# A hybrid layer whose engine queues are ordered by the scheduler's finer timeline model

## The chip, the cores and the metric

The kernel runs on one core of one Trainium2 chip. A core has engines that each work through a queue of their own, in order, and meet at semaphores: PE (TensorE, the matmuls), DVE (VectorE), ACT (ScalarE), POOL (GpSimd) and SP (SyncE, which here only issues DMA transfers). The metric is the device time of one launch in microseconds (us), the median over runs.

## The reference

One decoder layer, batch 1, 1024 tokens, width 1024, all float32. A cut of it:

```
def _hybrid_layer(x, ...):
    xn = _rmsnorm(x, norm1_g)
    proj = xn @ w_in                          # q, k, v (8 heads of 64) and u (512)
    q, k = _rmsnorm(q, q_norm_g), _rmsnorm(k, k_norm_g)
    attn = _dilated_attention(q, k, v)        # windows 128/512/2048, dilations 1/4/16
    ssm = _s5_mixer(u, ...)                   # 32 groups, 64 complex states each, then GELU and a gate
    mix = jnp.concatenate([_rmsnorm(attn, attn_out_norm_g), _rmsnorm(ssm, ssm_out_norm_g)], axis=-1)
    x = x + mix @ w_out
    hdn = jnp.square(jax.nn.relu(_rmsnorm(x, norm2_g) @ w_mlp_up))   # 1024 x 4096
    return x + hdn @ w_mlp_down                                      # 4096 x 1024
```

## The kernel before

Every large matrix product is made of three matmuls, because a float32 operand is split in a high and a low part: `split` (L76 to L78) writes the high part on ACT and then the low part on DVE, and `mm3` (L103 to L107) issues high by high (L105), high by low (L106) and low by high (L107), where "low" of the third is that of the operand which PE holds as weights. The first two matmuls of a product can therefore start when ACT has written the high part of the weights; the third needs DVE's low part.

The stages, in the order in which PE comes to them in the profile (times from the start of the span):

- 0 to about 73 us: the projection of u for 8 tiles of 128 tokens, beside the S5 parameters on DVE.
- to 222 us: the S5 mixer, in four quarters q. `ssm_main` loads a table D from d_kz (L393, on SP), makes psb on PE (L399), scans on DVE (L417), forms X (L425, L429; two of its products on POOL, L424 and L428), and sums psy on PE from D by U (L435) and X by ec (L438). GELU follows (L445 to L451, ending in z2), then a transpose (pszt, L461), a copy hz (L462) and a write to d_hz (L463, on SP). Woven into it is the projection of the first pair of heads: psq, 24 matmuls for each token tile and group of columns.
- 222 to 433 us: attention of pair p-1 beside the projection psq of pair p, for p from 1 to 3. In attention, pss are scores (L541), psp their transposes (L564), pt the split of these (L77 on ACT, L78 on DVE) and pso the product with V (L575).
- to 594 us: attention of the last pair, the gate, the output projection and the operands X0 to X6 of the MLP (t1 to t4 on L815 are sums that these are made of).
- 594 to about 892 us: the up projection in 16 blocks (`up_proj`, L853 to L920). A block loads its weights as two raw buffers of 512 KB (wm of the block, parts 0 and 1, L853 on SP), of which there are only two in all: part 0 of a block goes where part 0 of the block before was, as soon as that has been read for the last time. A block has seven products of 12 matmuls, in the order z, x, first y, T2 (into x's bank), B22 (into y's), T3 and T4 (into x's). Each takes one half of a tile wu for its split weights; five such tiles go round. L897, L902, L906 and L911 form the sums of weights on DVE, in place; T3's weights are the last that are read from part 0. After x, first y and T2 ACT copies the bank (L871, st from psx or psy), since later products add onto it.
- 892 to 1219 us: the down projection, on the same engines (`down_proj`; raw, ud, L969 to L980).

The order in the program text is not the order in the queues. The tile framework takes the instructions of the whole kernel, with their dependencies, and a scheduler in it lists them for each engine in the order in which its model of the engines says that they become ready. So the cost model of that scheduler is what sets the queues. Nothing changes at run time: an engine takes its list in order, and waits where the next instruction isn't ready.

## Time and profile before

| | us |
|---|---|
| median of 3 runs | 1217.33 (1213.23 to 1218.86) |
| the profiled execution | 1220.95 |
| its span (first to last instruction) | 1219.2 |

The profiled execution is 3.6 us above the median; 1.75 us of it lie outside its span. PE is the busiest engine, with 1139.4 us of the span. The rows further down come from this execution, and times in them count from the start of its span. "Busy" of PE is modelled, so a PE that is busy throughout may still run at half its clock: the granted clock stands in its own row or column (1.00 is 2.4 GHz, 0.50 is 1.2 GHz).

### The profile page before, as it was taken

How to read it: one execution, taken by the hardware profiler on the slowest of the kernel's cores; microseconds unless marked ns; L12 is line 12 of the kernel's file. 1: busy time of each engine (PE TensorE's matmuls, PEld its weight loads, DVE VectorE, ACT ScalarE, POOL GpSimd, SP SyncE). 2: the span in 40 equal slices, each digit the busy share in tenths (PEclk: the TensorE clock that was granted, in tenths of full speed). 3: DMA queues.
4: the chain of work that ended last, by engine and by line, in shares of the span. 5: the costliest groups of instructions: out<-in, count | busy, mean ns of one | idle time of the engine just before them, and what ended most of it. 6: DMA issues, size and time to landing. Idle time of an engine off the chain costs nothing.

```text
span 1219.2 us, 16630 instructions
## 1 busy us (share of the span) xinstructions
PE 1139.4 (93%) x5734; PEld 956.7 (78%) x5734; DVE 841.0 (69%) x1557; ACT 598.6 (49%) x1276; POOL 354.8 (29%) x528
## 2 busy tenths in 40 slices
PE   6766989999999999999999999999999999999998
PEld 4554777888898877787777888888878888888887
DVE  7999785567676777666876566665656775576763
ACT  5222233677776786533555555555544333333332
POOL 6685642354545445313312111122110000000000
PEclk9886887899999999999999999999999999999999
DMA  7734432635355425753244434434379999575930
GB/s 288 272 115 106 151 112 70 211 114 178 129 155 170 143 96 166 243 191 121 75 159 173 167 145 165 145 140 167 144 294 398 387 387 352 193 240 183 333 140 35
DMA packets 101093, 227.15 MB, mean 186 GB/s; under 512 B 8848, under 2 KB 27792, under 8 KB 96144
## 3 DMA queue, kind: packets, MB, share of 16 engines
q1 hardware_dynamic: 85136, 154.13, 37.2%
q0 software_dynamic: 14432, 69.22, 15.7%
q10 hardware_dynamic: 1440, 2.73, 0.6%
q8 instruction: 45, 0.74, 0.3%
q14 instruction: 40, 0.33, 0.1%
HBM read 168.93 MB, written 57.11 MB: 185 GB/s over the span
## 4 chain that ended last, share of the span: by engine, by line
PE 70%; DVE 11%; DMA 6%; issue 5%; POOL 4%; ACT 4%; SPq 0%; ACTq 0%; DVEq 0%; POOLq 0%
PE psx L105 7%; PE psx L106 7%; PE psx L107 7%; PE psy L105 7%; PE psy L106 7%; PE psy L107 7%; PE pso L575 3%; PE psq L107 2%; PE psq L105 2%; PE psq L106 2%; PE pss L541 2%; PE psp L564 2%; PE psy L438 1%; PE pso L107 1%; PE pso L105 1%
## 5 line engine op out<-in xcount | busy, mean ns | idle before, releaser
L77 ACT ACTIVATE ud<-raw 128x1024 fp32r<-128x1024 f32 x112 | 112.9, 1053 | 184.8 <-PE psy L107 81.0
L78 DVE TENSOR_TENSOR ud<-raw,ud 128x1024 fp32r<-128x1024 f32 x112 | 132.6, 1221 | 83.6 <-ACT ud L77 83.6
L105 PE MATMUL psx<-X,wu 128*128 128x512 f32 (+1 forms) x260 | 101.1, 389 | 4.5 <-ACT st L871 3.2
L106 PE MATMUL psx<-X,wu 128*128 128x512 f32 (+1 forms) x260 | 100.4, 386 | 0.7 <-DVE X L78 0.7
L107 PE MATMUL psx<-X,wu 128*128 128x512 f32 (+1 forms) x260 | 100.5, 386 | 0.5 <-DVE wu L78 0.5
L105 PE MATMUL psy<-ud 128*128 128x512 f32 x256 | 99.6, 389 | 0.0
L106 PE MATMUL psy<-ud 128*128 128x512 f32 x256 | 99.6, 389 | 0.0
L107 PE MATMUL psy<-ud 128*128 128x512 f32 x256 | 99.6, 389 | 0.0
L78 DVE TENSOR_TENSOR wu<-wm,wu 128x512 fp32r<-128x512 f32 x112 | 75.5, 701 | 30.8 <-ACT wu L77 30.6
L105 PE MATMUL psq<-wq,xt 128*128 128x384 f32 x256 | 93.7, 366 | 0.9 <-DMA xt<-d_x 0.8
L77 ACT ACTIVATE wu<-wm 128x512 fp32r<-128x512 f32 x112 | 66.7, 625 | 53.1 <-DMA wm<-in_w_up_dram 27.0
L106 PE MATMUL psq<-wq,xt 128*128 128x384 f32 x256 | 90.6, 354 | 0.5 <-DVE wq L82 0.5
L107 PE MATMUL psq<-wq,xt 128*128 128x384 f32 x256 | 90.8, 355 | 0.0
L875 POOL DMA_DIRECT2D d_a<-st x80 | 43.5, 544 | 130.1 <-DVE st L884 65.9
L106 PE MATMUL psx<-ud 128*128 128x512 f32 x192 | 74.8, 390 | 0.0
L105 PE MATMUL psx<-ud 128*128 128x512 f32 x192 | 74.7, 389 | 0.0
L107 PE MATMUL psx<-ud 128*128 128x512 f32 x192 | 74.7, 389 | 0.0
L980 DVE TENSOR_TENSOR raw<-raw 128x1024 f32<-128x1024 f32 x40 | 49.7, 1249 | 28.7 <-DMA raw<-in_w_down_dram 28.7
L549 POOL TENSOR_SCALAR s<-s,dn 128x128 f32<-128x128 f32 (+3 forms) x64 | 50.2, 787 | 47.9 <-DVE dn L548 45.9
L78 DVE TENSOR_TENSOR pt<-psp,pt 128x128 fp32r<-128x128 f32 (+2 forms) x96 | 51.1, 552 | 15.9 <-ACT pt L77 15.2
L105 PEld LDWEIGHTS psx<-X,wu 128*128 128x128 f32 x260 | 48.8, 188 | 16.5 <-ACT st L871 4.6
L575 PE MATMUL pso<-pt,V 128*128 128x256 f32 x320 | 54.6, 294 | 3.5 <-ACT pt L77 1.9
(294 smaller groups left out, 3012.5 us busy)
## 6 DMA issues: line engine op xcount, KB each, us to landing
raw<-in_w_down_dram SPq DMA_DIRECT2D x96, 512.0 KB, 9.0
xt<-d_x POOLq DMA_DIRECT2D x30, 1024.0 KB, 5.2
raw<-d_a SPq DMA_DIRECT2D x56, 512.0 KB, 8.1
d_a<-st POOLq DMA_DIRECT2D x80, 256.0 KB, 2.6
wm<-in_w_up_dram SPq DMA_DIRECT2D x32, 512.0 KB, 3.7
d_x<-xt POOLq DMA_DIRECT2D x8, 1024.0 KB, 5.1
d_a<-o POOLq DMA_DIRECT2D x32, 256.0 KB, 2.8
wq_r<-in_w_qkv_dram SPq DMA_DIRECT2D x16, 384.0 KB, 3.9
```

What stands on the lines that cost most here:

```text
L77: ACT.activation(h, src, AF.Copy)
L78: eng.tensor_tensor(l, src, h.bitcast(F32), op=OP.subtract)
L105: PE.matmul(ps, lhsT=ah, rhs=bh, start=start, stop=False, skip_group_check=more)
L106: PE.matmul(ps, lhsT=ah, rhs=bl, start=False, stop=False, skip_group_check=more)
L107: PE.matmul(ps, lhsT=al, rhs=bh, start=False, stop=stop, skip_group_check=more)
L438: PE.matmul(psy[s][:, a], lhsT=X[s * 64:s * 64 + 64, ri, a, :], rhs=ca[s * 64:s * 64 + 64, ri, a].rearrange("p d c -> p (d c)"), start=Fal ...
L541: PE.matmul(ps[:, :cw], lhsT=Qd[a][:, h, b * 128:(b + 1) * 128], rhs=K2[:, h, c0:c0 + cw], start=a == 0, stop=a == 1)
L549: POOL.tensor_scalar(s[:, :n], s[:, :n], dn, 1.0, op0=OP.mult, op1=OP.mult)
L564: PE.transpose(ps[:, kb * 128:(kb + 1) * 128], P[j][:, (k0 + kb) * 128:(k0 + kb + 1) * 128], ident)
L575: PE.matmul(po[:, :256], lhsT=V2[:, k0 + kb, h, :], rhs=pt[:, a, kb, :], start=k0 + kb == 0 and a == 0, stop=k0 + kb == nb - 1 and a == 1)
L875: POOL.dma_start(out=d_a[blk // 2][i][blk % 2], in_=st)
L980: DVE.tensor_tensor(rb, rb, raw_unit(wd(n, *b1)), op=op)
```

## The change

```
-    with tile.TileContext(nc) as tc:
+    with tile.TileContext(nc, schedule_with_timeline_sim=True) as tc:
         hybrid_layer_kernel(tc, io, out)
```

The scheduler uses another, finer model of the engines. The instructions are the same ones (5487 matmul rows on PE, 1557 on DVE, 1076 on ACT, 528 on POOL, 385 on SP, before and now), with the same shapes and dependencies; 4825 of PE's stand at another place in its queue (by up to 158 places), 1265 of DVE's, 735 of ACT's, 341 of POOL's and 143 of SP's. Buffer addresses can differ too. Three places follow.

PE in the up projection, block 4 (psx_7085 is its x, psx_6796 the x bank of block 2, psx_6940 that of block 3). Before, x of block 4 begins behind the last product (T4) of block 3:

```order
L105 MATMUL psx_6940<-X5_6001,wu_7063 128x512
L106 MATMUL psx_6940<-X5_6002,wu_7063 128x512
L107 MATMUL psx_6940<-X5_6001,wu_7063 128x512
L105 MATMUL psx_7085<-X0_5284,wu_7063 128x512
L106 MATMUL psx_7085<-X0_5285,wu_7063 128x512
L107 MATMUL psx_7085<-X0_5284,wu_7063 128x512
L105 MATMUL psx_7085<-X0_5284,wu_7063 128x512
```

Now it begins between T3 (weights wu_6854) and T4 (weights wu_6904) of block 2:

```order
L105 MATMUL psx_6796<-X6_5993,wu_6854 128x512
L106 MATMUL psx_6796<-X6_5994,wu_6854 128x512
L107 MATMUL psx_6796<-X6_5993,wu_6854 128x512
L105 MATMUL psx_7085<-X0_5284,wu_7063 128x512
L106 MATMUL psx_7085<-X0_5285,wu_7063 128x512
L105 MATMUL psx_6796<-X5_6001,wu_6904 128x512
L106 MATMUL psx_6796<-X5_6002,wu_6904 128x512
```

So the first product of block 4 moved from the end of block 3 to before the last product of block 2, and everything of block 3 that stood between now comes later.

ACT at the same place, where the rows read the same before and now (st_6851 is the copy of T2 of block 2, wm3_0 and wm3_1 the weights of block 3, wm4_0 those of block 4):

```order
L871 ACTIVATE st_6851<-psx_6796 128x512
L77 ACTIVATE wu_7020<-wm3_0_6899 128x512
L880 ACTIVATE st_6851<-st_6851 128x512
L881 ACTIVATE st_6851<-st_6851 128x512
L77 ACTIVATE wu_7063<-wm3_1_6901 128x512
L77 ACTIVATE wu_7063<-wm4_0_7044 128x512
```

That is the copy, the last read of wm3_0 on ACT, and, once wm4_0 has landed in its place, the split for x of block 4. These did not move among themselves; only PE's use of wu_7063 moved against them.

PE at the end of the S5 mixer (psq_1938 is a projection of the first pair of heads, psy0_1841 the last quarter's sum, X_1769 its X). Before, the projection is dealt out among the sums:

```order
L105 MATMUL psq_1938<-wq0_0_916,xt_1936 128x384
L106 MATMUL psq_1938<-wq0_0_916,xt_1936 128x384
L107 MATMUL psq_1938<-wq0_0_916,xt_1936 128x384
L438 MATMUL psy0_1841<-ec_1344,X_1769 128x128
L105 MATMUL psq_1938<-wq0_0_916,xt_1936 128x384
L106 MATMUL psq_1938<-wq0_0_916,xt_1936 128x384
L107 MATMUL psq_1938<-wq0_0_916,xt_1936 128x384
L438 MATMUL psy0_1841<-ec_1344,X_1769 128x128
```

Now all 24 of its matmuls stand ahead of the first sum with X_1769:

```order
L105 MATMUL psq_1938<-wq0_3_937,xt_1936 128x384
L106 MATMUL psq_1938<-wq0_3_937,xt_1936 128x384
L107 MATMUL psq_1938<-wq0_3_937,xt_1936 128x384
L438 MATMUL psy0_1841<-ec_1344,X_1769 128x128 x2
L435 MATMUL psy0_1841<-D_1723,U3_1643 128x128
L438 MATMUL psy0_1841<-ec_1344,X_1769 128x128 x2
```

Of psq_1938, 21 matmuls moved from behind that sum's start to before it.

DVE at the start of the up projection (t1, t2, t4, X1, X2 and X5 are operands of the last token tiles, raw_8782 a tile of the down projection, wm0 and wm1 the weights of blocks 0 and 1). Before:

```order
L815 TENSOR_TENSOR t1_6443<-psx_6428,b11s_6439 128x512
L906 TENSOR_TENSOR wm0_1_6465<-wm0_1_6465,wm0_0_6463 128x512
L815 TENSOR_TENSOR t2_6445<-psx_6434,t1_6443 128x512
L78 TENSOR_TENSOR wu_6530<-wm0_0_6463,wu_6530 128x512
L815 TENSOR_TENSOR t4_6447<-psx_6422,t2_6445 128x512
L78 TENSOR_TENSOR X2_5770<-psx_6434,X2_5769 128x512
L78 TENSOR_TENSOR wu_6565<-wm0_1_6465,wu_6565 128x512
L78 TENSOR_TENSOR X1_5380<-psx_6422,X1_5379 128x512
```

Now:

```order
L911 TENSOR_TENSOR wm0_0_6463<-wm0_1_6465,wm0_0_6463 128x512
L78 TENSOR_TENSOR wu_6530<-wm0_0_6463,wu_6530 128x512
L980 TENSOR_TENSOR raw_8782<-raw_8782,raw_8785 128x1024
L800 SCALAR_TENSOR_TENSOR xsn_6405<-x2_6359,rs2_6412,g2b_5723 128x512
L800 SCALAR_TENSOR_TENSOR xsn_6406<-x2_6360,rs2_6412,g2b_5723 128x512
L78 TENSOR_TENSOR wu_6565<-wm0_1_6465,wu_6565 128x512
L78 TENSOR_TENSOR wu_6615<-wm0_1_6465,wu_6615 128x512
L78 TENSOR_TENSOR wu_6565<-wm0_0_6463,wu_6565 128x512
L815 TENSOR_TENSOR t1_6443<-psx_6428,b11s_6439 128x512
L815 TENSOR_TENSOR t2_6445<-psx_6434,t1_6443 128x512
L78 TENSOR_TENSOR X2_5770<-psx_6434,X2_5769 128x512
```

Five items that stood behind t1 or further back (L911, the second low part of wu_6530, the sum on raw_8782, both parts of wu_6565 and one of wu_6615) moved ahead of it.

## Rows read from the trace of the kernel before

**Rows 1.** The page: engines, granted clock in 40 slices, the chain of waits.

```profile
PE 1139.4 (93%) x5734; PEld 956.7 (78%) x5734; DVE 841.0 (69%) x1557; ACT 598.6 (49%) x1276; POOL 354.8 (29%) x528
PEclk9886887899999999999999999999999999999999
PE 70%; DVE 11%; DMA 6%; issue 5%; POOL 4%; ACT 4%; SPq 0%; ACTq 0%; DVEq 0%; POOLq 0%
```

**Rows 2.** Stretches: us, then each engine's busy us (instructions), PEclk, DMA share, GB/s.

```profile
80.00:120.00 40.00, 24.26 (x172) 19.29 (x173) 38.27 (x49) 8.74 (x23) 26.00 (x29) 0.67 0.45 121
...
240.00:480.00 240.00, 229.74 (x1431) 206.45 (x1431) 172.01 (x474) 177.19 (x556) 121.30 (x199) 1.00 0.44 145
600.00:680.00 80.00, 75.54 (x337) 60.59 (x336) 56.23 (x85) 45.38 (x80) 16.84 (x27) 1.00 0.45 155
680.00:880.00 200.00, 200.00 (x884) 165.62 (x883) 129.34 (x204) 110.97 (x191) 40.77 (x76) 1.00 0.42 152
920.00:1160.00 240.00, 240.00 (x1060) 198.40 (x1059) 160.90 (x154) 88.49 (x88) 0.94 (x2) 1.00 0.86 306
```

**Rows 3.** One turn in block 3, all engines, in order of time (start, us).

```profile
690.80 0.39 PE L107 MATMUL psx<-X,wu 128*128 128x512 f32 x1
...
691.22 0.60 ACT L871 ACTIVATE st<-psx 128x512 f32<-128x512 f32 x1 [1.78 <-PE psx L107]
...
691.72 0.62 ACT L77 ACTIVATE wu<-wm 128x512 fp32r<-128x512 f32 x1
...
692.37 0.69 DVE L78 TENSOR_TENSOR wu<-wm,wu 128x512 fp32r<-128x512 f32 x1 [3.54 <-ACT wu L77]
...
693.09 0.33 SPq L853 DMA_DIRECT2D wm<-in_w_up_dram  x1
```

**Rows 4.** Landing of the weights' loads (line L853, 640 to 880 us).

```profile
DMA to landing us min/median/max: 3.1/3.6/6.3
```

**Rows 5.** Stretches of 5 us around the last quarter of the S5 mixer.

```profile
175.00:180.00 5.00, 2.12 (x14) 1.80 (x12) 3.85 (x7) 1.33 (x9) 4.08 (x4) 0.96 0.04 12
180.00:185.00 5.00, 5.00 (x30) 4.02 (x31) 1.89 (x4) 1.58 (x2) 1.86 (x3) 0.50 0.65 210
185.00:190.00 5.00, 5.00 (x46) 3.69 (x45) 1.54 (x4) 1.77 (x3) 0.11 (x1) 0.86 0.42 134
195.00:200.00 5.00, 2.08 (x13) 1.63 (x12) 3.85 (x6) 1.18 (x7) 4.36 (x3) 1.00 0.00 2
200.00:220.00 20.00, 20.00 (x66) 16.11 (x66) 8.18 (x23) 7.34 (x16) 4.08 (x7) 0.50 0.16 53
220.00:235.00 15.00, 13.12 (x80) 11.95 (x79) 7.67 (x24) 10.01 (x34) 5.14 (x11) 0.98 0.95 317
```

**Rows 6.** Matmuls there, at 195 us and at 219 us.

```profile
194.66 0.33 PE L105 MATMUL psq<-wq,xt 128*128 128x384 f32 x1
194.84 0.33 PE L106 MATMUL psq<-wq,xt 128*128 128x384 f32 x1
...
219.17 0.52 PE L106 MATMUL psq<-wq,xt 128*128 128x384 f32 x1
219.49 0.52 PE L107 MATMUL psq<-wq,xt 128*128 128x384 f32 x1
```

**Rows 7.** DVE at the start of the up projection, in order of time.

```profile
608.14 2.31 DVE L980 TENSOR_TENSOR raw<-raw 128x1024 f32<-128x1024 f32 x1
```

**Rows 8.** PE's waits, 594 to 660 us: us in total, times, longest.

```profile
PE psx L105 <- ACT st L871: 3.2, 3, 1.6
```

**Rows 9.** PE's waits in attention, 222 to 594 us.

```profile
PE pso L575 <- ACT pt L77: 1.9, 5, 0.6
...
PE pso L575 <- DVE pt L78: 1.3, 2, 1.1
```

**Rows 10.** Attention to 520 us by line and shape.

```profile
L78 DVE TENSOR_TENSOR pt<-psp,pt 128x512 fp32r<-128x512 f32 x48 | 32.0, 685 | 11.8 <-ACT pt L77 11.5
L77 ACT ACTIVATE pt<-psp 128x512 fp32r<-128x512 f32 x48 | 27.7, 600 | 6.2 <-PE psp L564 5.8
```

## Prediction

> **What bounds the kernel now.** I read the page first. PE is busy for 1139.4 us of the span of 1219.2, and the chain of waits lies on PE for 70% of it [rows 1]. So most of the time a new order can win or lose only by what PE itself loses: by gaps, and by stretches in which its clock is low. The next view is therefore the table of stretches. In the up projection (680 to 880 us) PE is busy for 200.00 us of 200 and in the down projection (920 to 1160) for 240.00 of 240, at a granted clock of 1.00 [rows 2]. Nothing can be won there by order; it can only be lost. In the main stretch of attention (240 to 480 us) PE is busy for 229.74 of 240, so the most that is to be had is 10.3 us [rows 2]. At the start of the up projection (600 to 680) it is 75.54 of 80: 4.5 us [rows 2]. The row of the granted clock is below 9 tenths in early slices only [rows 1], and the stretches of 5 us show what that is in the last quarter of the S5 mixer: 20 us at 0.50 without a gap, with gaps and other half-speed time ahead of it [rows 5]. There a good order has something to win. In the first 120 us I take no change: DVE's instructions are the same there and DVE, not PE, is full (38.27 of 40 from 80 to 120 [rows 2]).
>
> **The change part by part.** No instruction is added or removed. What counts is where each queue's next instruction isn't ready.
>
> (1) The up projection. Take block 4 as the order shows it. PE now begins x of block 4 after 22 matmuls from the end of T2 of block 2 (10 of the y product of block 3, 12 of T3 of block 2); before, 11 products of 12 lay between. Its weights come by a chain that did not move: T2's last matmul, ACT's copy of the bank, ACT's split of wm3_0 (the last read but one), DVE's low part, the transfer of wm4_0 into the place of wm3_0, ACT's split of wm4_0. The same chain, one block earlier, is in the trace: the last matmul of T2 starts at 690.80, the copy at 691.22, the split at 691.72, the low part at 692.37, and the transfer is issued at 693.09, which is 2.29 us after that matmul's start [rows 3]. It lands 3.6 us after the issue (median; 3.1 to 6.3) [rows 4], and the split takes 0.62 [rows 3]. So x's weights are ready 2.29 + 3.6 + 0.62 = 6.5 us after the start of T2's last matmul. PE is there after 23 steps of 0.226 us (884 matmuls in 200.00 us [rows 2]), which is 5.2 us. It waits 1.3 us, in order, with T4 of block 2 behind it, which is ready. With the landing at 3.1 it is 0.8, at 6.3 it is 4.0. The order has this for the even blocks from 4 to 14, six times; in the odd blocks the same count leaves about 1 us to spare. 6 x 1.3 = 8 us, from 5 to 24. Before, this cost nothing, since 132 steps (30 us) covered the chain. I take 8, as the median landing is the row nearest to it. That the transfers contend more when they are issued later I count at nothing: PE's rate, and with it theirs, stays the same.
>
> The Trainium skill ("DMA: Bandwidth & Descriptors", section "Anatomy of one DMA") fits a transfer by POOL's path as about 2.0 us and bytes over 436 GB/s, which for 512 KB makes 3.2 us, and the sum by it would be 6 x 0.9 = 5 us. The transfers here go by SP's path, and their median is 3.6 us [rows 4].
>
> (2) The start of the up projection. On DVE five groups of work now stand ahead of t1 and with it of X1, X2 and X5 of the last token tiles: L911, a low part of wu_6530, the sum on raw_8782, two low parts of wu_6565 and one of wu_6615. The sum took 2.31 us [rows 7], the others about 0.69 each, as the low part in [rows 3]: 2.31 + 5 x 0.69 = 5.8 us by which the last operands are later. PE needs them for the second halves of the first products. Of that comes back what PE lost there before, at most 4.5 us [rows 2], 3.2 of it on ACT's copy ahead of a later product [rows 8], because the copy and that product now stand farther apart. From 5.8 - 4.5 = +1 to 5.8: I take +3, in between, since only a part of the old loss lies on that copy.
>
> (3) The last quarter of the S5 mixer. The gaps and the half clock from 175 to 235 us are: 2.9 us idle before 180, 2.5 and 0.7 at a clock of 0.50 and 0.86, 2.9 idle from 195 to 200, 10.0 at 0.50 for 20 us, 1.9 idle to 235 [rows 5]; together 20.9 us, the most there is to win. The new order puts 21 matmuls of psq_1938 into the gap before the first sum with X_1769 (2.9 us idle [rows 5]), at 0.18 us each, 3.8 us [rows 6], and takes them out of the stretch at half clock, where 14 of them took 0.32 each [rows 6] and 7 at the end 0.18: 14 x 0.32 + 7 x 0.18 = 5.7 us off PE's path there. All of psb0 of that quarter now stands ahead of the sums of the quarter before, in the gap at 177 to 180 us, which gives up to 2.9 us. Against it, DVE has three low parts of the next pair's weights (3 x 0.6 us) ahead of the second half of X_1769. -5.7 - 2.9 + 1.8 = -7 us. The transfer of the attention's bias comes earlier by as much, as its place behind the last d_hz stays. The bounds are -20.9 and, if X comes late and PE idles as before, +2.
>
> What the clock does there is the open point. PE was busy for 20.00 us of 20 with the clock at 0.50 all through [rows 5], with sums (L435, L438) and psq mixed. "TensorE: Matmul & The Clock Gate" of the Trainium skill (section "The HAM clock gate") says that a PE which is idle falls to half its clock and that a busy one gets the full one back; by that, filling the gap at 196 us would keep the full clock, and the sum for this part would be near -20. The stretch that is busy at 0.50 does not agree, so I don't count on it; it is the first rival.
>
> (4) Attention beside the projection. Before, psq was dealt out in pieces of 1 to 12 matmuls between scores, transposes and products with V. Now whole groups of 24 stand together, and the attention in clusters between. Gains have the bound of 10.3 us. For losses: in nine places the order now puts the first pso less than 0.45 us of PE's work behind its psp, while the split between them takes 0.60 us on ACT and 0.69 on DVE [rows 10]; 9 x 1.29 = 11.6 us as the other end. Before, pso waited on pt for 1.9 us in 5 places and 1.3 in 2 [rows 9], so a place costs about 0.45: 9 x 0.45 = 4 us, less the old 3.2. I take +1.
>
> (5) The down projection: within a group of products the first matmuls of four banks now come before the second ones. All are ready, so 0.
>
> Sum: 8 + 3 - 7 + 1 = +5 us. On the profiled execution (1220.95 us, of which 1.75 outside its span) that is 1226; that execution was 3.6 above the median of the runs, so for the median I say 1217.33 + 5 = 1222 us.
>
> **The rivals.** First, on the other side: the last quarter of the S5 mixer keeps its full clock. Its price is the whole 20.9 us instead of 7, so 1222 - 14 = 1208 us. It decides from about 18 us on, as 12 us are lost elsewhere and 6 make a difference. For it speaks that PE now works through the gap ahead of the half-clock stretch; against it, that stretch's sums alone fill most of it, and nothing of them was made faster.
>
> Second: attention stalls in its clusters. 11.6 us instead of 1 gives 1233. For it speaks that ACT (177 us of 240) and DVE (172) have the attention's work to do in less time, if PE does its psq in one piece [rows 2]; against it, that scores of later blocks are now issued ahead and can be worked on during psq.
>
> Third: the order changes and PE's waits don't, in the up projection. If the loads are early enough there (the copy and split can start before their place, or another transfer takes 0.8 us less), part 1 is 0 and the time 1214. Against it, the landing has never been below 3.1 us, and 5.2 - 2.29 - 0.62 leaves 2.3.
>
> **How the numbers follow.** Chances: the sum as it stands 0.42, with 1212 to 1233 as its own range (part 1 at 5 to 13, part 2 at 1 to 6, part 3 at -12 to -3, part 4 at -2 to 5); full clock 0.20; stalls in attention 0.20; no stall in the up projection 0.18. This kernel's runs tell 0.5% from no change, or 6.1 us: faster is below 1211.2, slower above 1223.4. Of the sum's case I give 0.22 to slower, 0.17 to no change and 0.03 to faster; of the first rival 0.16 to faster, 0.03 to no change and 0.01 to slower; the second is slower; of the third 0.07 is faster and 0.11 no change. That is 0.26 faster, 0.31 no change, 0.43 slower. The range is 1203 to 1242: from the first rival with a few us gained in attention to the second with landings of the long kind.
>
> **What would show it.** Part 1: waits of PE at psx L105 on ACT's split of wu, about 1.3 us, six times, between 680 and 880 us, and PE's busy share there below 200 of 200; the loads of wm being what ACT waits for. No such waits would make it wrong. Part 2: DVE's sum on raw before L815 of the last tiles, and psz or psx waiting on X. Part 3: the granted clock from 195 to 220 us, and whether the first scores of attention come earlier. Part 4: PE busy from 240 to 480 us against 229.74. It would be wrong above all if PE's matmuls in the up projection start without gaps, or if the stretch at 0.50 is gone.

## The result and the profile after

The changed kernel takes 1278.94 us (median of 4 runs, 1277.53 to 1280.23); the kernel before took 1215.28 beside it (4 runs, 1211.28 to 1218.86). The ratio is 1.0525, with a 95% interval of 1.0485 to 1.0564: slower by 64 us. The forecast of 1222 us and its range up to 1242 are missed by far. The profiled execution took 1278.54 us against 1220.95, so 57.6 us are there to be found in the two traces.

The page after answers to [rows 1] (engines, granted clock in 40 slices, the chain):

```profile
PE 1162.4 (91%) x5734; PEld 970.9 (76%) x5734; DVE 833.3 (65%) x1557; ACT 593.5 (46%) x1276; POOL 359.3 (28%) x528
...
PEclk8977797899989999999999999999989999999999
...
PE 37%; issue 18%; DMA 9%; DVE 8%; POOL 5%; ACT 4%; SPq 0%; POOLq 0%; DVEq 0%; ACTq 0%
```

PE is idle for 1276.8 - 1162.4 = 114.4 us instead of 79.8, and its same 5734 rows take 23 us longer. The chain now lies on PE for 37% instead of 70%; 18% of it is "issue", time for which the profile shows no wait.

To see where, the two traces were laid beside each other at equal work of PE, counted in the columns that its matmuls have done. What the changed kernel is behind there is the lag (worked out from the starts in both traces; the left column is the time in the kernel before):

| point | lag, us | gained in the stage |
|---|---|---|
| start of attention, 231 us | -8.0 | -8.0 |
| 330 us | +7.7 | |
| 361 us | +19.4 | |
| 463 us | +32.1 | |
| 533 us, attention at its end | +41.7 | +49.7 |
| 600 us, MLP's start | +40.4 | -1.3 |
| 667 us, up projection begun | +41.8 | +1.4 |
| end of the up projection | +49.2 | +7.4 |
| down projection, throughout | +53.6 | +4.4 |
| end | +57.6 | +4.0 |

So attention is nearly the whole loss. Its stretch before, 230 to 497 us, and the one with as many matmul rows (1570) after, 222 to 536 us (columns as in [rows 2]; before first, then after):

```profile
230.00:497.00 267.00, 254.91 (x1570) 227.64 (x1571) 191.44 (x533) 195.62 (x606) 134.86 (x226) 1.00 0.46 153
```

```profile
222.00:536.00 314.00, 274.83 (x1570) 243.66 (x1569) 193.68 (x533) 197.07 (x608) 129.72 (x218) 0.95 0.39 131
```

The stretch is 47.0 us longer. PE's idle time goes from 12.1 to 39.2 us (+27.1); as many matmuls are busy for 19.9 us more, at a mean granted clock of 0.95 instead of 1.00. DVE and ACT work as long as before, in more time. Both parts start from waits. The waits of the engines beside PE in the stretch after, largest first, some rows left out (us in total, times, longest):

```profile
POOL s L549 <- DVE dn L548: 64.7, 30, 5.9
ACT pt L77 <- PE psp L564: 34.0, 23, 5.2
...
DVE s L543 <- PE psp L564: 19.4, 13, 3.7
...
ACT s L546 <- DVE mn L543: 14.7, 16, 2.1
```

and the same waits before:

```profile
POOL s L549 <- DVE dn L548: 45.2, 33, 6.2
...
ACT pt L77 <- PE psp L564: 12.6, 22, 1.2
...
ACT s L546 <- DVE mn L543: 3.9, 7, 1.3
```

ACT waits for PE's transposes for 34.0 us instead of 12.6, DVE for 19.4 (0.6 before), and PE for ACT's split for 9.0, the wait of [rows 9]. During 21.6 of ACT's 34.0 us and 11.4 of DVE's 19.4 PE was at work on psq (worked out from the starts and ends in the trace; before it was 4.3 of ACT's 12.6): while PE works through a long piece of psq, ACT and DVE run out of scores and transposes. That PE then wants at once what they haven't made is the reading of its own waits after, the six largest:

```profile
PE pso L575 <- ACT pt L77: 9.0, 8, 2.0
PE psp L564 <- DVE K L478: 7.2, 4, 5.4
PE psp L564 <- DVE pt L78: 5.2, 10, 1.5
PE psq L105 <- DVE V L512: 5.2, 1, 5.2
PE pss L541 <- DVE mn L543: 4.8, 9, 0.9
PE psn L520 <- POOL ssq L702: 1.4, 1, 1.4
```

Only the first was part of the forecast's counting. The third, ten times, is a transpose that must wait until DVE has read the former transpose out of the same PSUM bank. In the second and fourth, K and V are late because of other work ahead of them on ACT and DVE. One such stall can be read in the timeline (start, us, engine, operation, and in brackets the idle time before):

```profile
370.68 0.60 PE L564 MATMUL psp<-pack,s 128*128 128x128 f32 x4
...
373.70 1.06 ACT L77 ACTIVATE wg<-wg_r 128x1024 fp32r<-128x1024 f32 x1 [3.58 <-DMA wg_r<-in_glu_wp_dram]
...
374.79 1.23 DVE L78 TENSOR_TENSOR wg<-wg_r,wg 128x1024 fp32r<-128x1024 f32 x1 [4.47 <-ACT wg L77]
...
376.05 0.49 DVE L478 SCALAR_TENSOR_TENSOR K<-pst,pack,K 64x256 fp32r<-64x256 f32 x1
...
376.68 1.86 PE L564 MATMUL psp<-pack,s 128*128 128x128 f32 x7 [5.41 <-DVE K L478]
```

ACT stands 3.58 us before a split of weights (wg) whose transfer has not landed; DVE's next item is the low part of the same weights; K, which PE's next psp follows, stands behind it on DVE. PE waits 5.41 us behind a load that its next psp does not use. The clock around this stall, in stretches of 5 us:

```profile
365.00:370.00 5.00, 3.93 (x28) 3.17 (x27) 4.04 (x12) 3.21 (x9) 0.78 (x3) 1.00 0.86 288
370.00:375.00 5.00, 1.27 (x11) 1.04 (x10) 0.52 (x3) 1.42 (x4) 1.08 (x3) 0.88 0.64 218
375.00:380.00 5.00, 3.17 (x13) 2.32 (x13) 4.00 (x7) 4.15 (x23) 2.67 (x5) 0.50 0.33 105
380.00:385.00 5.00, 5.00 (x33) 5.00 (x32) 3.30 (x13) 3.32 (x11) 1.58 (x5) 0.94 0.01 3
```

With 3.7 us without work in one stretch the clock is at 0.50 in the next: this stall is paid once as idle time, and again in the matmuls behind it. "TensorE: Matmul & The Clock Gate" of the Trainium skill (section "HAM oscillation — how this bites in real kernels") describes this, waits between groups of matmuls that put the engine back to half its clock each time; for this stall the trace agrees, with 0.50 from 375 to 380 us. In the whole stretch of attention the clock is at 0.50 in eight pieces, with this sum (us in all, then PE's busy time in them):

```profile
sum 34.14, PE 29.57 PEld 26.68 DVE 21.89 ACT 22.30 POOL 13.72; mean PE 3.70 PEld 3.34 DVE 2.74 ACT 2.79 POOL 1.72
```

At the full clock that work would have taken no less than half, 14.8 us. So at most 14.8 of the 19.9 us by which the matmuls are longer are the clock; what the other 5 us are is not shown.

The up projection shows what the forecast said (stretches, answering to [rows 2]; then PE's waits from 594 to 960 us):

```profile
720.00:760.00 40.00, 39.16 (x172) 31.89 (x172) 23.75 (x38) 21.12 (x38) 7.53 (x14) 1.00 0.45 159
760.00:800.00 40.00, 38.96 (x173) 31.93 (x172) 24.47 (x39) 21.01 (x37) 7.53 (x14) 1.00 0.43 152
```

```profile
PE psx L105 <- ACT wu L77: 5.4, 6, 1.0
PE psy L105 <- ACT X L77: 2.4, 1, 2.4
PE psx L106 <- DVE X L78: 2.0, 1, 2.0
PE psx L105 <- DVE st L879: 1.6, 1, 1.6
PE psx L105 <- ACT ud L77: 1.1, 1, 1.1
```

PE waits six times at psx on ACT's split, 0.9 us each, and is busy for some 39.1 us of 40 where it had no idle time before. The next two rows are the start of the MLP, the last two the turn to the down projection: 2.7 of the 4.4 us there.

### The profile page after: what moved, and what is told of

Its sections match the earlier page's. It is cut to its first block, busy times and chain, and to the rows that moved or that the text cites. A ratio compares the mean times of both kernels' runs of the same rounds, so it can differ in the third digit from the quotient of the medians.

```text
span 1276.8 us, 16592 instructions
## 1 busy us (share of the span) xinstructions
PE 1162.4 (91%) x5734; PEld 970.9 (76%) x5734; DVE 833.3 (65%) x1557; ACT 593.5 (46%) x1276; POOL 359.3 (28%) x528
## 3 DMA queue, kind: packets, MB, share of 16 engines
q0 software_dynamic: 14432, 69.22, 14.8%
## 4 chain that ended last, share of the span: by engine, by line
PE 37%; issue 18%; DMA 9%; DVE 8%; POOL 5%; ACT 4%; SPq 0%; POOLq 0%; DVEq 0%; ACTq 0%
DMA raw<-in_w_down_dram 5%; POOL d_a L875 4%; PE psy L106 4%; PE psy L105 4%; PE psy L107 4%; PE psx L106 3%; PE psx L105 3%; PE psx L107 3%; PE psq L105 2%; PE psq L106 2%; PE psq L107 2%; PE pso L575 2%; PE pss L541 2%; DVE ud L78 1%; PE psp L564 1%
## 5 line engine op out<-in xcount | busy, mean ns | idle before, releaser
L106 PE MATMUL psy<-ud 128*128 128x512 f32 x256 | 99.7, 390 | 0.2 <-DVE ud L78 0.2
L107 PE MATMUL psy<-ud 128*128 128x512 f32 x256 | 99.6, 389 | 0.0
L105 PE MATMUL psq<-wq,xt 128*128 128x384 f32 x256 | 90.0, 352 | 10.3 <-DVE V L512 5.2
L106 PE MATMUL psq<-wq,xt 128*128 128x384 f32 x256 | 89.1, 348 | 6.5 <-DVE wq L82 6.5
L107 PE MATMUL psq<-wq,xt 128*128 128x384 f32 x256 | 88.1, 344 | 0.0
L105 PE MATMUL psy<-ud 128*128 128x512 f32 x256 | 84.7, 390 | 2.9 <-DVE x L997 2.9
L106 PE MATMUL psx<-ud 128*128 128x512 f32 x192 | 74.7, 389 | 0.0
L107 PE MATMUL psx<-ud 128*128 128x512 f32 x192 | 74.7, 389 | 0.0
L575 PE MATMUL pso<-pt,V 128*128 128x256 f32 x320 | 61.8, 314 | 11.2 <-ACT pt L77 9.7
L105 PE MATMUL psx<-ud 128*128 128x512 f32 x192 | 63.4, 390 | 1.1 <-ACT ud L77 1.1
L77 ACT ACTIVATE pt<-psp 128x128 fp32r<-128x128 f32 (+2 forms) x96 | 46.0, 494 | 37.8 <-PE psp L564 37.0
```

Source lines behind the costliest of these rows:

```text
L77: ACT.activation(h, src, AF.Copy)
L105: PE.matmul(ps, lhsT=ah, rhs=bh, start=start, stop=False, skip_group_check=more)
L106: PE.matmul(ps, lhsT=ah, rhs=bl, start=False, stop=False, skip_group_check=more)
L107: PE.matmul(ps, lhsT=al, rhs=bh, start=False, stop=stop, skip_group_check=more)
L575: PE.matmul(po[:, :256], lhsT=V2[:, k0 + kb, h, :], rhs=pt[:, a, kb, :], start=k0 + kb == 0 and a == 0, stop=k0 + kb == nb - 1 and a == 1)
```

## The experiments

All of them use one device. A list of instruction numbers is put into the kernel, and each is told to follow the one ahead of it on the same engine, without a semaphore; the scheduler then has no choice for them. It orders everything else anew around the list, though, and that moves much: with PE's old order in the changed kernel (the first run below), 362 of ACT's 456 instructions of attention stand at another place than in the changed kernel, and only 156 at another than in the kernel before. So no run below changes one queue alone. Each shows a held queue, with the other queues fitted to it by the finer model (base: changed) or by the old one (base: before). In the edits below the list stands in words; 2018 to 5701 are PE's instructions of attention, from the first scores on. The theories at the start were: (A) attention loses because PE's queue was changed there, psq above all; (B) it loses because the other engines' queues were. The expectations of the two fills and of the last two runs use A, B and C for other theories, which they state.

### Which queue, which stage

Old order of PE's queue in attention, the rest by the finer model:

```
     with tile.TileContext(nc, schedule_with_timeline_sim=True) as tc:
         hybrid_layer_kernel(tc, io, out)
+        hold(tc, nc)     # PE 2018 to 5701 in the order of before
```

> The changed kernel, with PE's queue in the attention stage (all PE instructions traced from the first scores to the last product with V) held to the order of before; the scheduler's finer model still orders everything else. By stretches of equal PE work, the changed kernel loses 47 us between the first scores and the end of attention, 8 us in the up projection, about 10 us at the two ends of the down projection, and gains 5 to 8 us in the S5 mixer. Theory A (PE's place in the queue: projection matmuls stand in whole groups of 24 and attention in clusters, so the other engines' answers are not covered) expects 1279 - 40 to 47, that is 1232 to 1240 us. Theory B (the other engines' queues: weight splits and copies that wait for a transfer stand ahead of attention's work on ACT and DVE) expects little, 1268 to 1279 us.

1248.4 us, ratio to before 1.0263 [1.0223, 1.0304]: 30 us given back, which lies between the two ranges. Behind the first scores the lag stays between -3 and +3 up to 463 us and then grows to +9.5 at 533, where the last pair of heads meets the output projection. From -6 at 231 us, that is 16 of attention's 50 us that are still lost.

Old order of the other four engines there instead:

```
+        hold(tc, nc)     # DVE, ACT, POOL, SP: attention in the order of before
```

> The changed kernel, with the queues of ACT, DVE, POOL and SP in the attention stage held to the order of before, and PE's left to the finer model. Theory A expects little, since the clusters on PE stay if the model still makes them: 1268 to 1279 us. Theory B expects 1232 to 1240 us. A third way: the model puts PE's queue where the others' queues allow, so PE's order goes back with them and both theories gain; then PE's order must be read beside the time.

1290.75, 1.0612 [1.0566, 1.0659]: 12 us worse than the change alone, and outside both ranges. PE's queue is a third one here: 1436 of its 1676 instructions of attention stand at another place than in the changed kernel, and eleven whole groups of 24 psq matmuls stand together (nine in the changed kernel, none in the kernel before). (B) falls: with the other four queues exactly as before in attention, nothing came back.

PE's old order from the scores through the output projection:

```
+        hold(tc, nc)     # PE, scores to the operands of the MLP, order of before
```

> The changed kernel, with PE's queue held to the order of before from the first scores through the gate, the output projection and the operands of the MLP (the run before held it to the last product with V, and lost 10 us behind the third pair). If PE's order is the cause there too, 1248 - 8 to 12, that is 1236 to 1240 us, and what stays above 1217 is the up projection and the two ends of the down projection, 15 to 20 us. If the other queues are the cause there, 1245 to 1250 us.

1254.02, 1.0311 [1.0267, 1.0355]. A miss: with the list going on through the output projection nothing more comes back than in the first run, so what grows there is not PE's order.

The kernel before with the new order of all queues ahead of attention:

```
     with tile.TileContext(nc) as tc:
         hybrid_layer_kernel(tc, io, out)
+        hold(tc, nc)     # all engines, up to attention, new order
```

> The kernel before, with all five queues of the part ahead of attention (projection of u, S5 mixer, first pair's projection) held to the order of the changed kernel. If the 5 to 8 us that the changed kernel is ahead by at the first scores are its order's, and attention takes them over: 1207 to 1211 us, faster than before. If they are lost again because attention starts later than its projection anyway: 1213 to 1217 us.

1216.97, 1.0002 [0.9982, 1.0021]. In its trace PE is 6.2 us ahead at 231 us, and 35 us later 1.6: attention takes it back, 2.7 us of it in one wait (222 to 260 us):

```profile
PE psq L105 <- DMA xt<-d_x: 2.7, 1, 2.7
```

At its end this trace is 5.6 us ahead again, but of an execution of the kernel before that was itself 3.6 us above its median; the medians decide.

PE's old order in the MLP, the rest by the finer model:

```
+        hold(tc, nc)     # PE, MLP, order of before
```

> The changed kernel, with PE's queue of the MLP (up and down projection) held to the order of before. If the 8 us of the up projection (six waits of about 1 us for the weights of every second block, and smaller ones) and the 4 to 10 us at its end and at the end of the down projection are due to PE's order: 1279 - 10 to 18, that is 1261 to 1269 us. If the transfers or the other queues set these waits, 1272 to 1279 us.

1279.77, 1.0533 [1.0484, 1.0582]. The lag stays flat through the up projection, its 7.4 us are gone, and come back at the start of the down projection as one wait of PE, 960 to 1040 us:

```profile
PE psx L105 <- ACT ud L77: 7.9, 1, 7.9
```

That split of ACT stood behind a load that came late:

```profile
999.29 1.06 ACT L77 ACTIVATE ud<-raw 128x1024 fp32r<-128x1024 f32 x1 [15.57 <-DMA raw<-d_a]
```

So PE's order does set the waits of the up projection, as the first range assumed, and the time is still close to the second: what was gained there was lost behind a load. The reverse, the kernel before with PE's new order in the up projection only:

```
+        hold(tc, nc)     # PE, products of the up projection, new order; base: before
```

> The kernel before, with only PE's queue of the up projection held to the order of the changed kernel. There the changed kernel loses 7.4 us between blocks 2 and 15, 5.4 of it in six waits of x for the weights of every second block (the term of 8 us in the forecast). If that is PE's order alone: 1217 + 5 to 9, that is 1222 to 1226 us, with six waits of about 1 us. If it needs the new order of ACT and DVE too: 1215 to 1219 us.

1232.87, 1.0141 [1.0116, 1.0166]: +17 us, a miss of both ranges. Its waits of PE from 594 to 920 us:

```profile
PE psz L105 <- ACT wu L77: 7.0, 2, 6.8
PE psx L105 <- ACT wu L77: 5.6, 6, 1.1
PE psx L105 <- DVE st L879: 2.3, 1, 2.3
```

The second row is the term that was forecast, isolated: six waits of 0.9 us. The others stand at the start and the end of the stage (609 and 907 us), where PE's new order meets the old model's ahead and behind; a wait of 6.8 us is not in the change itself.

### What in PE's order of attention

In the kernel before psq's matmuls stand in 107 pieces among attention's, with never more than 27 others between two; in the changed kernel in 47, nine of them of 24 or more, with up to 64 others between. (The expectations say 52 for the changed kernel: there, neighbouring groups count apart, by which the kernel before has 110.) Three runs change the kernel before: psq gathered in 24s where the first of each group stood, then in 12s, then PE's whole new order. A fourth deals psq out evenly in the changed kernel.

```
+        hold(tc, nc)     # PE 2018 to 5701: order of before, psq in 24s (base: before)
```

> The kernel before, with PE's queue of the attention stage as before but for one thing: the 24 projection matmuls of each group (psq) are gathered where the first of them stood. Nothing else changes places with each other. Before, they stand in 107 pieces, at most 27 other PE instructions apart; in the changed kernel in 52 pieces, up to 64 apart. Theory A1 (grouping the projection, so that attention has nothing beside it, is the cause) expects 1240 to 1262 us. Theory A2 (the order among attention's own instructions is the cause) expects 1217 to 1230 us.

1264.55, 1.0384 [1.0337, 1.0431], 3 us above the range of A1.

```
+        hold(tc, nc)     # the same, psq in 12s
```

> The kernel before, as in the run that gathered 24 projection matmuls, but gathered in halves of 12, each where its first one stood. If the loss grows with the length of the stretches of attention that are left without projection, about half of the 47 us: 1230 to 1245 us. If any gathering breaks the weave, 1255 to 1265 us.

1243.15, 1.0227 [1.0196, 1.0259]. Pieces of 12 cost 28 us, of 24 cost 47: gathering psq is enough to lose as much as the change loses in attention, and more the longer the pieces are.

```
+        hold(tc, nc)     # PE 2018 to 5701, new order (base: before)
```

> The kernel before, with only PE's queue of the attention stage held to the order of the changed kernel; the old scheduler orders all else. The reverse of the run that held PE's old order there (1248 us, 30 less than the changed kernel). Theory A (PE's order in attention is the cause) expects 1217 + 30 to 47, that is 1247 to 1264 us. If the loss needs the changed order of the other queues or of the stages ahead as well, 1217 to 1235 us.

1292.48, 1.0621 [1.0579, 1.0662]: +75 us, 28 above the range of (A). PE's new order is enough for the loss, and costs more under the old model than in the change. Its largest wait of PE (222 to 560 us):

```profile
PE pss L541 <- DVE mn L543: 27.5, 28, 3.5
```

```
+        hold(tc, nc)     # PE 2018 to 5701: new order, psq dealt out in 436 pieces (base: changed)
```

> The changed kernel, with PE's queue of the attention stage in its own new order but for one thing: the projection matmuls are dealt out again among the attention instructions behind them (436 pieces, 0.87 for each instruction of attention, at most 28 held back). Theory A1 expects 15 to 40 us back: 1239 to 1264 us. Theory A2 expects 1265 to 1285 us, since attention's own order is still the new one.

1276.59, 1.0481 [1.0432, 1.053]: 2 us better than the change, within the range of A2. This spoke against psq as the whole cause, so psq's places and attention's own steps were separated: where psq stands, and in which order scores, transposes and products with V fill the other places.

```
+        hold(tc, nc)     # psq's places of before, attention's own steps in new order (base: before)
```

> The kernel before; in PE's queue of the attention stage the projection matmuls stay where they were, and the places between them are filled with the attention instructions in the order of the changed kernel. Gathering the projection alone cost 47 us, and the whole new order on PE 75 us. If the two parts add (theory A3), attention's own new order costs 75 - 47 = 28 us: 1240 to 1250 us. If attention's own order costs something only where no projection stands beside it, 1217 to 1225 us.

1272.8, 1.0464 [1.0431, 1.0497].

```
+        hold(tc, nc)     # the same queue of PE (base: changed)
```

> The changed kernel with the same PE queue in the attention stage as the run before this one: projection matmuls at the places that they had before, attention instructions in the new order, the finer model for all other queues. Dealing them out one by one brought 2 us, restoring the whole old order 30. Theory A3 (two parts that add) expects about half of the 30 back: 1259 to 1269 us. If only the grouping counts and the one-by-one deal was a bad one, 1245 to 1252 us. If the changed kernel's loss is attention's own order, 1275 to 1280 us.

1275.03, 1.048 [1.0447, 1.0514]. The first of the two missed both its ranges: attention's own new order costs 57 us by itself. The second lies at the edge of its third range: psq's old places give back 4. So the loss of the changed kernel looked like attention's own order, until the last two runs.

Next, the short distances on PE were lengthened in the changed kernel, with psq pulled forward as filler; its trace shows whether the targeted waits shrink.

```
+        hold(tc, nc)     # PE 2018 to 5701, new order, psq pulled ahead of psp and pso (base: changed)
```

> The changed kernel, with one edit of PE's queue in attention (222 to 536 us of the profile after): where a transpose (psp) stands too close behind the former user of its PSUM bank, or a product with V (pso) too close behind the transpose whose split it reads, matmuls of the projection psq that stand further back are pulled forward to fill the gap. By PE's own work in the order, the distance from a psp to the next psp in its bank is under 1.3 us in 7 places instead of 13 (none in the kernel before), and from a psp to its first pso under 0.5 us in 5 places instead of 9, under 1.2 us in 17 instead of 26 (15 before). Theory A, that attention's loss of 47 us is made of these short distances: about half of what exceeds the kernel before is removed, so 12 to 24 us less than the changed kernel's 1279, 1255 to 1267 us, with PE's waits of psp on pt and pso on pt at half of 5.2 and 9.0 us. Theory B, that the loss comes from the order of scores, transposes and products of different heads among themselves (the engines waiting for each other in turn), and that distances on PE only show where it surfaces: 1272 to 1282 us.

1331.73, 1.0961 [1.0923, 1.0998].

```
+        hold(tc, nc)     # the same, another choice of places
```

> The same edit with another choice of places: the distance from a psp to the next psp in its bank is under 1.3 us in 9 places instead of 13, and from a psp to its first pso under 0.5 us in 5 instead of 9, under 1.2 us in 13 instead of 26 (15 in the kernel before). So the products with V are back at the old count of short distances, and the banks mostly are not. Theory A with both kinds of distance counting alike: 1255 to 1267 us, as its neighbour; if the products with V were the larger part, 3 to 8 us below its neighbour; if the banks were, 3 to 8 us above it. Theory B: 1272 to 1282 us, like its neighbour.

1319.6, 1.0856 [1.0828, 1.0885]. Both theories missed, by 38 us and more. PE's waits in the first of the two, 222 to 590 us:

```profile
PE psq L105 <- DVE V L512: 60.0, 12, 8.0
PE pss L541 <- DVE mn L543: 7.4, 9, 2.8
PE pso L575 <- ACT pt L77: 4.5, 5, 1.9
PE psp L564 <- DVE pt L78: 4.3, 7, 1.2
```

The two waits that were aimed at did shrink (9.0 to 4.5, 5.2 to 4.3). But a psq group that begins earlier waits for its bank, which DVE frees when it copies the former group into V: 60 us. The scheduler did move V forward on DVE, 19 of 32 by up to 16 places, but not enough. So the run says nothing on what the short distances cost; it says that psq pulled forward waits for something else.

The last two runs fill the missing corner, psq's places new, attention's own steps in the old order:

```
+        hold(tc, nc)     # psq's new places, attention's own steps as before (base: changed)
```

> The changed kernel; in PE's queue of attention the places of the projection's matmuls (psq) are the new ones, and what stands between them (scores, transposes, products with V) is in the old order among itself. With three earlier runs it makes a table of two by two in the changed kernel: both new 1279, psq's places old 1275, both old 1248. Theory A (the two parts add): attention's own order is the costly part, so 1279 - 1275 + 1248 = about 1252 us. Theory C (the two parts belong together: each order is tuned so that the pieces of psq stand where attention would wait, and with the other's places the short distances fall where nothing fills them; from a psp to its first pso under 1.2 us in 38 places here, against 26 with both new and 15 with both old): no gain, 1270 to 1295 us.

1302.94, 1.0727 [1.0691, 1.0763], 51 us above (A) and 8 above the range of (C).

```
+        hold(tc, nc)     # the same queue of PE (base: before)
```

> The kernel before, with the same queue of PE as its neighbour: psq at the new places, attention's own steps in the old order. The table in the kernel before: both old 1215, attention's own order new 1273, both new 1292. Theory A (the parts add): 1215 + 1292 - 1273 = about 1235 us. Theory C (each order fits its own places): 1265 to 1290 us, as for its neighbour, since there are as many short distances in it as in the others or more.

1286.44, 1.0578 [1.0545, 1.0611], in the range of (C). Together, in us:

| what orders all but PE's attention | own steps old, psq old | own new, psq old | own old, psq new | both new |
|---|---|---|---|---|
| the old model | 1215 | 1273 | 1286 | 1292 |
| the finer model | 1248 | 1275 | 1303 | 1279 |

In the first row the two halves cost 57 and 71 us and both together 75, not 128. In the second, own steps back to old costs 24 where psq stays new, and saves 27 where psq is old too. The parts don't add: no gain, as (C) said, against (A) in both kernels. What is shown is that attention's loss comes with PE's queue there: PE's old order gives back 30 us, its new one costs 75 in the kernel before, and the old order of the other four gives back nothing. Shown too is that the loss can't be divided between psq's places and attention's own steps: either new half alone costs 71 and 57 us. Why an order of attention's steps and the pieces of psq between them fit each other or don't is argued and not shown, since the other queues were fitted anew each time. The waits that lead differ: scores behind mn with the whole new order (27.5 us above) and with the other four queues held (10.4), psq behind V in the fills, and in the rest psp behind DVE's reading of its bank or pso behind ACT's split, as here in the last run (230 to 560 us):

```profile
PE psp L564 <- DVE pt L78: 14.0, 12, 3.5
PE pso L575 <- ACT pt L77: 13.9, 15, 2.5
PE psp L564 <- DVE K L478: 11.8, 7, 4.4
```

Not settled is how the loss in the changed kernel divides between the bank of psp, the split that pso waits for, and the clock that sinks after stalls; no run took one of them away without making another wait. No run had PE's new order with the other queues exactly as they were before. Nor is it shown what in the finer model gives the long pieces of psq. No version beat the kernel before.

## Why the prediction was wrong

**Part 4, attention, is the step that failed.** It said +1, with a ceiling of 11.6; measured are +49.7 (lag) or 47.0 (stretch). The step was the bound on what the clusters cost. The mechanism was that of the second rival, with a chance of 0.20 and 1233 us, but its price was bounded wrongly, in three ways that the trace can be held against. First, the ceiling counted one kind of wait, pso behind its psp, at nine places of 1.29. That kind came out at 9.0 us in 8 places, up to 2.0 each, so this count alone was nearly right as a ceiling, but it was then discounted to 4 by taking the 0.45 us that a place cost before [rows 9]; it came out at 1.1. Second, it left out the other things that a cluster waits for: the bank of the former psp (5.2 us in 10 places), scores behind mn (4.8 in 9), K and V held up behind other work (12.4): together 22.4 us, where the same waits had been 4.9. In the order, worked out with PE's own durations, a psp follows the former one in its bank within 1.3 us in 13 places, in none before; that count was to be had blind. Third, it took the clock as 1.00 whatever PE lost: the same matmuls took 19.9 us longer, up to 14.8 of them because of 34.1 us at 0.50, none of which were there before. The argument against that rival, that scores issued ahead can be worked on during psq, is refuted by ACT's 34.0 us of waiting for psp and DVE's 19.4, most of it while PE was on psq: they ran dry.

**Part 1, the up projection, was right.** Six waits at psx on ACT's split, at x of blocks 4 to 14, 0.9 us each instead of 1.3, with ACT waiting for the loads of wm; 5.6 us of the 8 when isolated, 7.4 by the lag. The landing of the weights' loads is 3.8 us in the median after. The third rival (no stalls there) falls.

**Part 2** was +3, the lag grows by 1.4 at the MLP's start, within the bounds given, and PE waits there for X, as its sign said (2.4 and 2.0 us above).

**Part 3, the S5 tail,** was -7; the lag at the start of attention is -8.0. That the numbers agree is luck: what came earlier by then is mostly psq, and not the stage's own work. Its last transposes start when they did, here before and after:

```profile
222.53 1.04 PE L461 MATMUL pszt<-pack,z 128*128 128x128 f32 x8
```

```profile
222.57 1.03 PE L461 MATMUL pszt<-pack,z 128*128 128x128 f32 x8
```

ACT stood before its copy of them (hz), V came late behind that, and PE waited for V, so that most of the lead was gone:

```profile
223.20 2.20 ACT L462 ACTIVATE hz<-pszt 128x512 f32<-128x512 f32 x2 [6.61 <-PE pszt L461]
...
231.82 0.69 PE L105 MATMUL psq<-wq,xt 128*128 128x384 f32 x1 [5.16 <-DVE V L512]
```

So the term was no saving, and the kernel before with just this order is at a ratio of 1.0002. The working followed PE to the end of the stage and did not ask whether attention's start could use the lead. The first rival, the full clock, falls in the stretch that it spoke of; ahead of it the clock is full where it was half:

```profile
175.00:180.00 5.00, 4.29 (x41) 3.30 (x39) 4.97 (x7) 2.76 (x11) 4.83 (x5) 1.00 0.33 77
180.00:185.00 5.00, 5.00 (x54) 3.96 (x52) 1.21 (x3) 1.66 (x3) 0.57 (x3) 1.00 0.72 282
...
195.00:200.00 5.00, 1.31 (x6) 0.87 (x6) 4.97 (x8) 1.41 (x9) 4.42 (x7) 0.97 0.44 140
200.00:220.00 20.00, 19.96 (x76) 16.75 (x77) 8.52 (x27) 8.37 (x16) 3.12 (x5) 0.58 0.40 137
```

The gap at 175 to 180 us is nearly filled (4.29 us busy, [rows 5] had 2.12), and the 5 us behind it run at 1.00 instead of 0.50, which the working had not counted. The gap ahead of the last sums is still there (1.31 us busy of 5, [rows 5] had 2.08), and the clock behind it is 0.58 instead of 0.50. The first sum with X_1769 did start earlier, at 196.76 instead of 199.57 us, but PE had run through psq by then, and waited a second time, 2.06 us, for the other half of X, which stands behind three low parts of weights on DVE. By the prediction's own count of idle time and half clock, 175 to 235 us lose about 21 us after as before.

**Part 5** was 0. The down projection itself is flat at a lag of 53.6, but its start and the kernel's end gave 4.4 and 4.0 us, the latter mostly one wait (from 1200 us on):

```profile
PE psy L105 <- DVE x L997: 2.9, 1, 2.9
```

## What to carry to other kernels

Where two kinds of work share PE, compare first in two orders how long the pieces are in which the filler is dealt out, and how the dependent steps between them stand: here gathering psq, which had mostly stood in pieces of 1 to 12, in pieces of 12 and 24 cost 28 and 47 us, and a new order of attention's own steps with psq's places untouched cost 57. When bounding what a new order can lose, count every distance in it that another engine must bridge, the reuse of a PSUM bank and what stands ahead on the other engines' queues among them, and add the clock that follows a stall. A piece of another order can't be priced alone: the costs of the two halves did not add in either row of the table. And before saying what a held queue isolates, read the other queues too: here the scheduler moved them with it.

## What was not expected of the hardware

- A stall of 5.4 us left PE at half clock behind it [375 to 380 us: 0.50], and over attention the clock was at 0.50 for 34.1 us, in 29.6 of which PE was busy: up to 14.8 us were paid again on top of 27.1 us of added idle time.
- A lead of 6 to 8 us at the start of attention vanished in some 35 us of it, in both kernels that had one: with one wait of 5.16 us for V in the changed kernel, and one of 2.7 us for a load in the other.
- One load can hold up three engines: ACT stood 3.58 us before the split of wg, DVE 4.47 us, and PE 5.41 us, for a transpose that does not read wg.
